# Unscaled first transposes, aligned buffers, later gate sums, 128-row rotary scores and second modulation vectors from the first stage on, in a hybrid attention block

## The chip, the cores and the metric

The kernel runs on one core of a Trainium2 chip. The metric is the device time of one execution in microseconds (us). Engines are named as in the profile: PE (TensorE: matmuls; PEld are its weight loads), DVE (VectorE), ACT (ScalarE), POOL (GpSimd), SP (SyncE, which issues most DMAs). L12 is line 12 of the kernel that a row belongs to; the changed kernel has line numbers of its own.

## The reference

One block over 256 latent tokens `x` and 256 context tokens `ctx`, width 2048, in float32. In short:

```python
sh1, sc1, gt1, sh2, sc2, gt2 = split(silu(c) @ w_mod + b_mod, 6)       # and the same of c_ctx
h  = rmsnorm(x, g_attn) * (1 + sc1) + sh1                                # hc of ctx likewise
cq, ckv, kr, qn, kn, vn, f = split_columns(h @ w_in)                     # and of hc
o_mla = 8 heads: scores of (128 plain + 64 rotary) columns over 512 keys, softmax, values
o_na  = 4 heads of neighbourhood attention with a bias, plus the context keys
o_fn  = Fourier mixing of f in 4 groups
x  = x + gt1 * (concat(o_mla, o_na, o_fn) @ w_out)
h2 = rmsnorm(x, g_ffn) * (1 + sc2) + sh2
u  = depthwise_conv3(h2 @ w_up) + conv_b                                 # 2 x 5632 columns
x  = x + gt2 * ((silu(gate(u)) * val(u)) @ w_down)
return rmsnorm(x, g_final)
```

`w_mod` alone is 2048 x 12288: its first third feeds the first modulation (sh1, sc1), the rest, 67 MB, the gates and the second modulation.

## The kernel before

Every float32 operand of a large product is kept as two fp32r limbs, H (the rounded value, made by ACT, L123) and L (the rest, made by DVE, L124); `split` makes them. A product is then three matmuls, H·H, H·L and L·H (`mm3`, L108 to L111). Weights arrive over SP's queue as `raw` tiles of 1 MB, in the list `order`, some tiles ahead, and are split by quarters into `hl` tiles.

The stages, in the order in which PE goes through them:

- First stage (to about 146 us). `x` and `ctx` come in four tiles of 128 tokens; each is squared and summed on ACT (L299), its rstd is made (L105, L106), the tile is scaled (L301) and transposed by PE (L364, with the identity from `sm`, a constant tile that comes by DMA) into `xT`. Then for each of 16 blocks `g` of 128 channels: `mod1_mm(g)` multiplies silu(c) by 2 MB of `wm1` (L318, into the bank `ms`), ACT copies the sums (`part`, L321), `mod1_h(g)` transposes them (L326), DVE adds them up (`mt`, L330) and the modulated block is written as limbs into `hx` and `hc`; and `g1(g)` accumulates seven output tiles over the channels with `wA`. `mod1_mm(g)` and `mod1_h(g)` are written among the tiles of `g1(g - 1)`; the tile framework orders each engine's instructions by priorities and dependences.
- V, B, NA (to 282 us), F, FN and MLA (to 440): the other projections, neighbourhood attention, Fourier mixing, MLA. In MLA the query of a pair of heads is `q[:, limb, i, :]`: i = 0, 1 are the two heads' plain columns, i = 2 their 64 rotary columns one above the other. A rotary score is an `mm3` with 64 rows of q and of the key `krH`, `krL`.
- O (to 522): the output projection `wo`, in four blocks of 512 columns; `x2_cols` (L742, L743) adds the gated result to x, `h_cols` transposes it (L754) into `h2`, scaled by `A2`. `h2` has two columns more than tokens, which hold the limbs of `B2`.
- UP and DN in four chunks (to the end): the MLP's first matmuls read `h2` with those columns (258 wide). After eight of them `hn`, the finished input, is there, and `up_mm2` runs two matmuls per weight tile: L834 multiplies the weight's H by both limbs of `hn` at once (512 wide), L835 its L by H (256 wide). DN (`at`, then `x2_cols` again) uses `mm3` with 512 columns.

Beside this runs the second modulation, `m2`: 128 tiles `wm2` of 0.5 MB, issued by POOL (L221) into 4 buffers, each multiplied by one element of silu(c) per partition and accumulated on DVE (L234, L236) into `acc`, 16 tiles to a block of 1024 columns, the blocks in the order gate 1, sc2/sh2, gate 2. `paced(n)` counts PE's columns, and with `RATES` of the stage calls `fill()`: one DMA more, one accumulation more, and `m2_sum()` if a block is complete. For a gate block, `m2_end` splits `acc` into limbs `acl` and `m2_sum` sums it over the partitions with a matrix of ones (L270, L271); for the others, eight matmuls of two columns (L260) go to `b2v`, from which `A2` and `B2` are made. `fill_to(n)` finishes n tiles: 64 ahead of `A2`, 96 ahead of `B2` and the added columns of `h2`, 112 and 128 in DN. From the 97th tile on, a small copy on POOL (`hold`, L216) that reads a weight's fresh limb stands ahead of the DMA.

Large tiles share sixteen buffers of 8256 bytes (`b8`), sized by `h2`'s 258 columns.

Of the kernel before, what the change touches and what calls it, by code (L numbers as in the profile page):

```python
# [33 lines left out]
RATES = dict(V=0.647, B=0.336, NA=0.237, F=0.135, FN=0.464, MLA=0.292, O=0.226, UP=0.132, DN=0.428)  # L34
# [18 lines left out]
def block_kernel(ctx: ExitStack, tc: tile.TileContext, a, out):  # L53
# [13 lines left out]
    def b8(shape, dt=F32, s="b8"):  # L67
        return sp.tile(shape, dt, tag="b8", bufs=16, name=nm(s))
# [39 lines left out]
    def mm3(ps, lH, lL, rH, rL, first, last, skip=False):  # L108
        pe.matmul(ps, lH, rH, start=first, stop=False, skip_group_check=skip)  # L109
        pe.matmul(ps, lH, rL, start=False, stop=False, skip_group_check=skip)  # L110
        pe.matmul(ps, lL, rH, start=False, stop=last, skip_group_check=skip)  # L111
        paced(3 * rH.shape[-1])

# [67 lines left out]
    def take(key, i):  # L181

        n = quarters.index((key, i))
        while st[1] <= min(n + look[0], len(quarters) - 1):
# [7 lines left out]
            ins = split(t[:, 0, :hs], t[:, 1, :hs], raws[k][:, o : o + hs])  # L192
# [60 lines left out]
    def m2_sum():
        if m2["due"] is None:
            return
# [12 lines left out]
        for h in range(2):  # L268
            ps = bank()
            pe.matmul(ps, ones_r, v[h][:, 0, :], start=True, stop=False)  # L270
            pe.matmul(ps, ones_r, v[h][:, 1, :], start=False, stop=True)  # L271
# [24 lines left out]
    act.dma_start(rope, a["rope"])
    for t in range(4):
        junk = b8([P, D], s="junk")
        act.activation(junk, xt[t], AF.Square, accum_out=ssx[:, t : t + 1])  # L299
        rstd(rx[:, t : t + 1], ssx[:, t : t + 1], D)  # L300
        dve.tensor_scalar(xt[t], xt[t], rx[:, t : t + 1], None, ALU.mult)  # L301
    act.activation(c1, smv("c1"), AF.Silu)
# [8 lines left out]
    def mod1_mm(g):  # L311

        for q in range(2):
            w = raw_tile(("m", g, q), 6)
            w = w.rearrange("p (k n) -> p k n", k=8)
            for k in range(8):
                r = 32 * (k % 4)
                pe.matmul(ms[r : r + 32, 0:256], cs[:, 8 * q + k, :], w[:, k, :], start=(q == 0 and k < 4),  # L318
                          stop=(q == 1 and k >= 4), tile_position=(0, r))
# [4 lines left out]
    def mod1_h(kt, sb):  # L324
        for s in range(2):
            pe.transpose(ms[:, 256 + s * P : 256 + (s + 1) * P], sb[:, s * P : (s + 1) * P], ident)  # L326
        t = tiny(4, "mt")
        tv = t.rearrange("p (s j) -> p s j", s=2)
        quarters_ = ms[:, 256:512].rearrange("p (s r c) -> p s c r", s=2, r=4)[:, :, 0:2, :]
        dve.tensor_reduce(tv, quarters_, AX.X, ALU.add)  # L330
        dve.tensor_tensor(tv, tv, bm1[:, kt], ALU.add)
        dve.scalar_tensor_tensor(tv[:, 1], tv[:, 1], 1.0, ga[:, kt], ALU.add, ALU.mult)
        m = kt // 4
        if hx[m] is None:
# [15 lines left out]
    def g1(kt, tiles):  # L350
        for i in tiles:
# [5 lines left out]
            mm3(accs[i][:, SEQ:], lH, lL, *hsl(hc, kt), first=False, last=(kt == KT - 1), skip=True)  # L357

    for t in range(4):
        for m in range(4):  # L360
            ps = bank()
            for k in range(4):
                kt = 4 * m + k
                pe.transpose(ps[:, k * P : (k + 1) * P], xt[t][:, kt * P : (kt + 1) * P], ident)  # L364
            (act.copy if m % 2 else dve.tensor_copy)(xT[m][:, :, t * P : (t + 1) * P],
                                                     ps.rearrange("p (k q) -> p k q", k=4))
# [59 lines left out]
    def rope_T(ps, H, L):  # L426
# [5 lines left out]
        split(H, L, r)  # L432
# [3 lines left out]
    rope_T(ps[:, :SEQ], krH[:, :SEQ], krL[:, :SEQ])  # L436
# [610 lines left out]
```

## Time and profile before

| | us |
|---|---|
| median of three runs | 1277.49 (1276.57 to 1278.4) |
| profiled execution | 1279.01 |
| span in the profile | 1277.2 |
| PE busy | 1243.7 (97%) |
| PE weight loads (beside matmuls) | 1069.2 (84%) |
| DVE busy | 978.6 (77%) |
| ACT busy | 699.0 (55%) |
| POOL busy | 111.5 (9%) |
| DMA | 304.81 MB, mean 239 GB/s |

PE is busy nearly all the time. A matmul's end is modelled in the profile, and matmuls overlap at their ends, so the distance from one start to the next tells what a matmul costs, and its mean duration (ns) moves with that distance. In rows of waits the releaser is the instruction that came last.

### The profile page before, as it was taken

What the parts mean: (1) busy time and instruction counts of PE and PEld (TensorE: products, weight loads), DVE (VectorE), ACT (ScalarE), POOL (GpSimd) and SP (SyncE); (2) the same over time, 40 slices, a digit from 0 to 9 for tenths busy, and PEclk for the clock granted to TensorE, in tenths of its full rate; (3) what the DMA queues carried; (4) which work ended last, traced back from release to release, by engine and by line L of the source; (5) the groups of instructions that cost most, each with busy time, mean ns of one, the idle gap of its engine ahead of it and who ended that gap; (6) DMA issues with size and microseconds to landing.
All of it is one profiled execution on the core that took longest, in us unless ns stands there. A gap on an engine that the chain in (4) does not pass through costs nothing.

```text
span 1277.2 us, 19956 instructions
## 1 busy us (share of the span) xinstructions
PE 1243.7 (97%) x7536; PEld 1069.2 (84%) x7536; DVE 978.6 (77%) x1757; ACT 699.0 (55%) x1343; POOL 111.5 (9%) x177
## 2 busy tenths in 40 slices
PE   5999999999999999999999999999999999999996
PEld 4888879898787888999988878888888888888885
DVE  5444588999989788899989975777766677777785
ACT  5333323765555555576666544666654566556663
POOL 0000121111111002200121500000000000000000
PEclk9999999999999999999999999999999999999999
DMA  9998689677756977754767857544455645564531
GB/s 387 419 397 327 223 305 323 231 243 249 258 194 232 368 294 270 261 227 165 286 226 253 320 204 264 212 162 169 165 198 180 249 165 183 184 227 165 172 125 66
DMA packets 53648, 304.81 MB, mean 239 GB/s; under 512 B 6064, under 2 KB 7216, under 8 KB 26800
## 3 DMA queue, kind: packets, MB, share of 16 engines
q1 hardware_dynamic: 34256, 234.37, 49.7%
q0 software_dynamic: 18432, 67.12, 15.5%
q10 hardware_dynamic: 864, 2.05, 0.4%
q8 instruction: 59, 0.97, 0.3%
q14 instruction: 37, 0.30, 0.1%
HBM read 301.42 MB, written 2.10 MB: 238 GB/s over the span
## 4 chain that ended last, share of the span: by engine, by line
PE 90%; DMA 3%; DVE 3%; issue 1%; ACT 1%; POOL 0%; DVEq 0%; ACTq 0%; POOLq 0%
PE ps L834 21%; PE ps L109 16%; PE ps L110 15%; PE ps L111 15%; PE ps L835 11%; DMA wm<-in_wm_dram 3%; PE g L109 2%; PE ms L318 2%; PE g L110 2%; PE g L111 2%; DVE acc L236 1%; DVE hl L124 1%; PE ps L493 1%; PE ps L364 1%; DMA sm<-in_small_dram 1%
## 5 line engine op out<-in xcount | busy, mean ns | idle before, releaser
L123 ACT CAST hl<-raw 128x512 fp32r<-128x512 f32 (+2 forms) x732 | 444.0, 611 | 359.8 <-PE ps L111 191.1
L124 DVE TENSOR_TENSOR hl<-raw,hl 128x512 fp32r<-128x512 f32 (+2 forms) x732 | 485.8, 677 | 172.6 <-ACT hl L123 166.4
L834 PE MATMUL ps<-hn,hl 128*128 128x512 f32 x1152 | 404.3, 395 | 0.0
L835 PE MATMUL ps<-hn,hl 128*128 128x256 f32 x1152 | 323.4, 281 | 0.0
L834 PEld LDWEIGHTS ps<-hn,hl 128*128 128x128 f32 x1152 | 216.4, 188 | 51.2
L835 PEld LDWEIGHTS ps<-hn,hl 128*128 128x128 f32 x1152 | 217.1, 188 | 0.2
L236 DVE SCALAR_TENSOR_TENSOR acc<-wm,c,acc 128x1024 f32<-128x1024 f32 x120 | 153.6, 1280 | 8.7 <-DMA wm<-in_wm_dram 8.4
L110 PE MATMUL ps<-hl,act 128*128 128x512 f32 x344 | 135.7, 394 | 0.5 <-DVE hl L124 0.5
L109 PE MATMUL ps<-hl,act 128*128 128x512 f32 x344 | 135.2, 393 | 0.0
L111 PE MATMUL ps<-hl,act 128*128 128x512 f32 x344 | 135.2, 393 | 0.0
L221 POOL DMA_DIRECT2D wm<-in_wm_dram x128 | 68.3, 534 | 310.7 <-DVE acc L236 233.8
L110 PEld LDWEIGHTS ps<-hl,act 128*128 128x128 f32 x344 | 64.7, 188 | 15.9 <-DVE hl L124 1.5
L109 PEld LDWEIGHTS ps<-hl,act 128*128 128x128 f32 x344 | 64.6, 188 | 14.9
L111 PEld LDWEIGHTS ps<-hl,act 128*128 128x128 f32 x344 | 64.7, 188 | 14.6
L109 PE MATMUL ps<-h,hl 128*128 128x258 f32 x256 | 72.5, 283 | 0.0
L111 PE MATMUL ps<-h,hl 128*128 128x258 f32 x256 | 72.1, 282 | 0.0
L110 PE MATMUL ps<-h,hl 128*128 128x258 f32 x256 | 72.1, 282 | 0.0
L216 POOL COPY hold<-hl 128x1 f32<-128x1 f32 x36 | 36.0, 999 | 286.7 <-DVE hl L124 286.7
L109 PE MATMUL ps<-hl,mix 128*128 128x512 f32 x128 | 50.5, 394 | 0.0
L110 PE MATMUL ps<-hl,mix 128*128 128x512 f32 x128 | 50.1, 391 | 0.0
L111 PE MATMUL ps<-hl,mix 128*128 128x512 f32 x128 | 49.9, 390 | 0.0
L855 ACT ACTIVATE cv<-ps,sm 128x256 f32<-128x256 f32 x88 | 49.4, 564 | 0.5
(282 smaller groups left out, 2143.2 us busy)
## 6 DMA issues: line engine op xcount, KB each, us to landing
raw<-in_wup_dram SPq DMA_DIRECT2D x88, 1024.0 KB, 5.1
wm<-in_wm_dram POOLq DMA_DIRECT2D x128, 512.0 KB, 5.1
raw<-in_wdn_dram SPq DMA_DIRECT2D x44, 1024.0 KB, 4.9
raw<-in_wm_dram SPq DMA_DIRECT2D x32, 1024.0 KB, 14.4
raw<-in_wo_dram SPq DMA_DIRECT2D x16, 1024.0 KB, 9.9
raw<-in_wB_dram SPq DMA_DIRECT2D x10, 1024.0 KB, 7.4
raw<-in_wA_dram SPq DMA_DIRECT2D x8, 896.0 KB, 14.5
x<-in_x_dram SPq DMA_DIRECT2D x4, 1024.0 KB, 8.8
```

What stands on the lines that cost most here:

```text
L109: pe.matmul(ps, lH, rH, start=first, stop=False, skip_group_check=skip)
L110: pe.matmul(ps, lH, rL, start=False, stop=False, skip_group_check=skip)
L111: pe.matmul(ps, lL, rH, start=False, stop=last, skip_group_check=skip)
L123: act.copy(H, src)
L124: return dve.tensor_tensor(L, src, H.bitcast(F32), ALU.subtract).ins
L216: hold = pool.tensor_copy(tiny(1, "hold"), recent[0][:, 1, 0:1].bitcast(F32)).ins
L221: pool.dma_start(w, a["wm2"][blk * 16 + kt])
L236: dve.scalar_tensor_tensor(m2["a"], w, c1[:, kt : kt + 1], m2["a"], ALU.mult, ALU.add)
L318: pe.matmul(ms[r : r + 32, 0:256], cs[:, 8 * q + k, :], w[:, k, :], start=(q == 0 and k < 4), stop=(q == 1 and k >= 4), tile_position=(0, r))
L834: pe.matmul(ps, w[:, 0, k * P : (k + 1) * P], h[:, :, k, :], start=kt == 0, stop=False, skip_group_check=True)
L835: pe.matmul(ps[:, :SEQ], w[:, 1, k * P : (k + 1) * P], h[:, 0, k, :], start=False, stop=kt == KT - 1, skip_group_check=True)
L855: act.activation(t, ps[:, :SEQ], AF.Identity, bias=c[:, 3:4], scale=c[:, 1:2])
```

## The change

- x and ctx come in eight half tiles. Their transposes take them unscaled, with an identity `idt` made on the chip by POOL. The square sums make one joint rms: a matmul with ones spreads it over the partitions (`rxb`), and each block of `xT` is multiplied by it on DVE in `mod1_h`. `sm`, `rope` and `c1` come later. All copies out of PE's transposes are DVE's.
- `issue_after` pins orders: the first modulation's matmuls behind the transposes, the joint matmul behind `mod1_mm(0)`, each later `mod1_mm` behind the last `g1`. `G1_CUT` is 2. The tiles of `wA` come as two halves.
- `RATES` has an entry A: some 12 `wm2` tiles are loaded and accumulated in the first stage; V, B and NA have lower rates; F to DN are as before.
- A gate block's limbs are two tiles of 1024 columns, and its sum waits for six more calls of `m2_sum` (`SUM_LAG`) or for `fill_to`.
- The buffers are 12 of `b8` (8192 bytes) and 4 of `h8` (8448 bytes, for `h2`, x, q, k and others). `hn` is stored by channel block, then limb, so that L834's 512 columns are one run.
- A rotary query is stored with H in one half of the partitions and L in the other, for each head; a score takes two matmuls of 128 rows (with `krH`, `krL`, which hold the key twice) instead of three of 64.

```diff
-RATES = dict(V=0.647, B=0.336, NA=0.237, F=0.135, FN=0.464, MLA=0.292, O=0.226, UP=0.132, DN=0.428)
+RATES = dict(A=0.17, V=0.45, B=0.2, NA=0.16, F=0.135, FN=0.464, MLA=0.292, O=0.226, UP=0.132, DN=0.428)
...
     def b8(shape, dt=F32, s="b8"):
-        return sp.tile(shape, dt, tag="b8", bufs=16, name=nm(s))
+        return sp.tile(shape, dt, tag="b8", bufs=12, name=nm(s))
+    def h8(shape, dt=F32, s="h8"):
+        return sp.tile(shape, dt, tag="h8", bufs=4, name=nm(s))
...
     def m2_end(blk, acc):
         if KIND[blk // 2] != "g":
-            m2["due"] = (blk, acc)
+            m2["due"], m2["age"] = (blk, acc), SUM_LAG
             return
...
+        H, L = [sp.tile([P, 1024], F32R, tag="acc", bufs=3, name=nm("acl")) for _ in range(2)]
+        split(H, L, acc)
+        m2["due"], m2["age"] = (blk, (H, L)), 0
+
+    def m2_sum(now=False):
+        m2["age"] += 1
+        if m2["due"] is None or not (now or m2["age"] > SUM_LAG):
             return
...
     def fill_to(n):
-        while m2["acc"] < n or m2["due"]:
+        while m2["acc"] < n:
             fill()
+        m2_sum(True)
...
+    def x_in():
+        for t in range(4):
+            for h in range(2):
+                junk = sp.tile([P, 1024], F32, tag="acc", bufs=3, name=nm("junk"))
+                last = act.activation(junk, xt[t][:, h * 1024 : (h + 1) * 1024], AF.Square,
+                                      accum_out=ssx[:, 2 * t + h : 2 * t + h + 1]).ins
+                for m in (2 * h, 2 * h + 1):
+                    ps = bank()
+                    for k in range(4):
+                        kt = 4 * m + k
+                        pe.transpose(ps[:, k * P : (k + 1) * P], xt[t][:, kt * P : (kt + 1) * P], idt)
+                    copied = dve.tensor_copy(xT[m][:, :, t * P : (t + 1) * P], ps.rearrange("p (k q) -> p k q", k=4)).ins
+        x_made.extend([last, copied])
+        with tc.issue_after(last):
             act.dma_start(sm, a["small"])
...
+        ps = bank()
+        with tc.issue_after(m_mm[0]):
+            x_made.append(pe.matmul(ps, ones, dgs, start=True, stop=True).ins)
+        x_made[0] = act.copy(rxb, ps).ins
...
+            if g:
+                held.enter_context(tc.issue_after(g1_last[-1]))
...
+            dve.tensor_tensor(xk, xk, rxb, ALU.mult)
...
+    def qr_limbs(q):
+        def limbs(src):
+            for i, hs in enumerate(halves):
+                act.copy(q[hs, i, 2, :], src[hs])
+            for i, hs in enumerate(halves):
+                dve.tensor_tensor(q[halves[1 - i], i, 2, :], src[hs], q[hs, i, 2, :].bitcast(F32), ALU.subtract)
+        return limbs
...
-            mm3(ps, q[hs, 0, 2, qs], q[hs, 1, 2, qs], krH[hs, :], krL[hs, :], False, True)
+            pe.matmul(ps, q[:, i, 2, qs], krH, start=False, stop=False)
+            pe.matmul(ps, q[:, i, 2, qs], krL, start=False, stop=True)
...
-    h2 = [b8([P, 2, 4, SEQ + 2], F32R, s="h2") for _ in range(4)]
+    h2 = [h8([P, 2, 4, SEQ + 8], F32R, s="h2") for _ in range(4)]
...
-        hn.append(b8([P, 2, 4, SEQ], F32R, s="hn"))
+        hn.append(b8([P, 4, 2, SEQ], F32R, s="hn"))
...
-                pe.matmul(ps, w[:, 0, k * P : (k + 1) * P], h[:, :, k, :], start=kt == 0, stop=False, skip_group_check=True)
+                pe.matmul(ps, w[:, 0, k * P : (k + 1) * P], h[:, k].rearrange("p s n -> p (s n)"), start=kt == 0, stop=False, skip_group_check=True)
```

In the order of the instructions this shows at three places. The first is PE at the end of the transposes of x. Before (`raw_41` to `raw_46` are tiles of `wm1`, two to a block; `part` the copied sums):

```order
L364 MATMUL ps_33_209<-sm_64,x_8_90 128x128 x4
L318 MATMUL ms_17_118<-raw_41_222,cs_72 32x256 x8
L318 MATMUL ms_17_118<-raw_42_224,cs_72 32x256 x8
L326 MATMUL ms_17_118<-sm_64,part_49_254 128x128 x2
L318 MATMUL ms_17_118<-raw_44_228,cs_72 32x256 x8
L318 MATMUL ms_17_118<-raw_45_230,cs_72 32x256 x8
L326 MATMUL ms_17_118<-sm_64,part_58_294 128x128 x2
L318 MATMUL ms_17_118<-raw_46_232,cs_72 32x256 x8
```

PE there, after (L347 is the joint rms, `g1_0` the first accumulator of `g1`):

```order
L327 MATMUL ps_39_215<-idt_72,x_8_93 128x128 x4
L367 MATMUL ms_15_108<-raw_9_96,cs_74 32x256 x8
L367 MATMUL ms_15_108<-raw_10_98,cs_74 32x256 x8
L347 MATMUL ps_46_252<-dgx_45_250,ones_r_68 128x512
L379 MATMUL ms_15_108<-idt_72,part_43_244 128x128 x2
L116 MATMUL g1_0_47_255<-hx_55_269,hl_59_279 128x256
```

Two and a half blocks of the modulation stood ahead of the first `g1` matmul; now one does, with the joint matmul.

The second is PE in V, around the first gate sum (`acl` the accumulator's limbs, `hl` a quarter of a V weight). Before:

```order
L109 MATMUL ps_197_1619<-hl_230_1798,hx_159_1270 128x512
L110 MATMUL ps_197_1619<-hl_230_1798,hx_159_1270 128x512
L111 MATMUL ps_197_1619<-hl_230_1798,hx_159_1270 128x512
L270 MATMUL ps_246_1898<-acl_240_1877,ones_r_68 128x512
L271 MATMUL ps_246_1898<-acl_240_1877,ones_r_68 128x512
L270 MATMUL ps_247_1902<-acl_241_1880,ones_r_68 128x512
L271 MATMUL ps_247_1902<-acl_241_1880,ones_r_68 128x512
L109 MATMUL ps_198_1620<-hl_230_1798,hc_160_1271 128x512
```

PE in V after:

```order
L116 MATMUL ps_217_1690<-hl_245_1858,hx_176_1314 128x512
...
L118 MATMUL ps_218_1691<-hl_245_1858,hx_176_1314 128x512
...
L118 MATMUL ps_219_1692<-hl_245_1858,hc_177_1315 128x512
L286 MATMUL ps_257_1949<-acl_239_1830,ones_r_68 128x512
L287 MATMUL ps_257_1949<-acl_240_1831,ones_r_68 128x512
L286 MATMUL ps_258_1953<-acl_239_1830,ones_r_68 128x512
L287 MATMUL ps_258_1953<-acl_240_1831,ones_r_68 128x512
```

The sum now stands behind nine matmuls with `hl_245`; on DVE the limbs `acl` are made two instructions ahead of that `hl_245`.

The third is the seam between `wo` and the MLP. PE before (`acc_729` is the block of sh2, `hl_849` the last `wo` weight, `x2_743` the second half of the tokens, `hl_851` a weight of the MLP):

```order
L111 MATMUL ps_823_5234<-hl_837_5304,mix_541_3737 128x512
L260 MATMUL ps_845_5353<-ones_r_68,acc_729_4666 128x2 x8
L109 MATMUL ps_824_5235<-hl_837_5304,mix_541_3737 128x512
...
L111 MATMUL ps_824_5235<-hl_849_5372,mix_684_4454 128x512
L754 MATMUL ps_862_5438<-sm_64,x2_743_4759 128x128
L754 MATMUL ps_863_5447<-sm_64,x2_743_4759 128x128
L109 MATMUL ps_867_5481<-h2_745_4766,hl_851_5383 128x258
```

PE after:

```order
L118 MATMUL ps_821_5234<-hl_839_5349,mix_682_4459 128x512
L826 MATMUL ps_852_5416<-sm_64,x2_738_4746 128x128
...
L826 MATMUL ps_853_5425<-sm_64,x2_739_4747 128x128
L276 MATMUL ps_862_5454<-ones_r_68,acc_773_4929 128x2 x8
L116 MATMUL ps_866_5489<-h2_740_4753,hl_842_5363 128x258
```

The sum of the block of sh2 stood inside the `wo` matmuls; now it stands between the last of them and the first MLP matmul. On POOL, before, a `hold` copy and a DMA take turns:

```order
L221 DMA wm2_805_5104<-in_wm2_dram 128x1024
L216 COPY hold_810_5139<-hl_809_5129 128x1
L221 DMA wm2_811_5141<-in_wm2_dram 128x1024
L216 COPY hold_827_5245<-hl_826_5238 128x1
L221 DMA wm2_828_5247<-in_wm2_dram 128x1024
```

POOL after (`wm2_849` is the 96th tile, the last that the sum of `acc_773` needs; `hl_848` is a quarter of an MLP weight):

```order
L239 DMA wm2_840_5359<-in_wm2_dram 128x1024
L234 COPY hold_854_5435<-hl_848_5387 128x1
L234 COPY hold_856_5440<-hl_848_5387 128x1
L234 COPY hold_858_5445<-hl_848_5387 128x1
L234 COPY hold_860_5450<-hl_848_5387 128x1
L239 DMA wm2_849_5400<-in_wm2_dram 128x1024
L239 DMA wm2_855_5437<-in_wm2_dram 128x1024
```

Four copies that read one MLP weight now stand in a row ahead of the last DMA of the 96.

More of the change, by code (lines that the diff above doesn't have):

```diff
@@ L110, in mm3 @@
         pe.matmul(ps, lH, rL, start=False, stop=False, skip_group_check=skip)
-        pe.matmul(ps, lL, rH, start=False, stop=last, skip_group_check=skip)
+        ins = pe.matmul(ps, lL, rH, start=False, stop=last, skip_group_check=skip).ins
         paced(3 * rH.shape[-1])
+        return ins
     def paced(n):
@@ L191, in take @@
             t = quarter(k)
-            ins = split(t[:, 0, :hs], t[:, 1, :hs], raws[k][:, o : o + hs])
+            with ExitStack() as held:
+                if k == ("A", 0):
+                    for made in x_made if q < 2 else (hx_made[-1], hmade[-1]):
+                        held.enter_context(tc.issue_after(made))
+                ins = split(t[:, 0, :hs], t[:, 1, :hs], raws[k][:, o : o + hs])
             hls[k, q] = recent[0] = t
@@ L293, in block_kernel @@
         xt.append(x_)
-        if t == 0:
-            act.dma_start(sm, a["small"])
[L296 to L302, printed above, removed]
+    emit_dma(order.index(("m", 1, 1)))
+    hmade, hx_made, g1_last, m_mm, x_made = [], [], [], [], []
@@ L311, in mod1_mm @@
     def mod1_mm(g):
[L313 to L319, printed above, removed]
+        with ExitStack() as held:
+            if g:
+                held.enter_context(tc.issue_after(g1_last[-1]))
+            for q in range(2):
+                w = raw_tile(("m", g, q), 6)
+                w = w.rearrange("p (k n) -> p k n", k=8)
+                for k in range(8):
+                    r = 32 * (k % 4)
+                    ins = pe.matmul(ms[r : r + 32, 0:256], cs[:, 8 * q + k, :], w[:, k, :], start=(q == 0 and k < 4),
+                                    stop=(q == 1 and k >= 4), tile_position=(0, r)).ins
+                m_mm.append(ins)
         sb = b1(s="part")
@@ L324, in mod1_h @@
     def mod1_h(kt, sb):
[L325 to L330, printed above, removed]
+        with ExitStack() as held:
+            for made in g1_last[-1:] if kt else x_made[1:]:
+                held.enter_context(tc.issue_after(made))
+            for s in range(2):
+                pe.transpose(ms[:, 256 + s * P : 256 + (s + 1) * P], sb[:, s * P : (s + 1) * P], idt)
+            t = tiny(4, "mt")
+            tv = t.rearrange("p (s j) -> p s j", s=2)
+            quarters_ = ms[:, 256:512].rearrange("p (s r c) -> p s c r", s=2, r=4)[:, :, 0:2, :]
+            dve.tensor_reduce(tv, quarters_, AX.X, ALU.add)
         dve.tensor_tensor(tv, tv, bm1[:, kt], ALU.add)
@@ L356, in g1 @@
             mm3(accs[i][:, :SEQ], lH, lL, *hsl(hx, kt), first=(kt == 0), last=(kt == KT - 1), skip=True)
[L357 to L366, printed above, removed]
+            g1_last.append(mm3(accs[i][:, SEQ:], lH, lL, *hsl(hc, kt), first=False, last=(kt == KT - 1), skip=True))
+    x_in()
+    sb0 = mod1_mm(0)
+    x_rms()
     accs = [bank(f"g1_{i}") for i in range(N_A)]
     for g in range(KT):
+        if g == 0:
+            mod1_h(0, sb0)
+            continue
+        if g == 1:
+            g1(0, range(0, 4))
+            with tc.issue_after(hx_made[-1]):
+                act.dma_start(rope, a["rope"])
+                act.activation(c1, smv("c1"), AF.Silu)
+            pace[0] = RATES["A"]
         sb = mod1_mm(g)
-        if g:
-            g1(g - 1, range(0, G1_CUT))
+        n = 5 if g == 1 else G1_CUT
+        g1(g - 1, range(4 if g == 1 else 0, n))
         mod1_h(g, sb)
-        if g:
-            g1(g - 1, range(G1_CUT, N_A))
+        g1(g - 1, range(n, N_A))
     g1(KT - 1, range(N_A))
@@ L431, in rope_T @@
         dve.tensor_tensor(r, r, sw, ALU.add)
-        split(H, L, r)
+        limbs(r)
+    def qr_limbs(q):
[5 more added lines that the diff above has]
+        return limbs
     ps = bank()
     proj_T(("B", 1), ps, True)
-    rope_T(ps[:, :SEQ], krH[:, :SEQ], krL[:, :SEQ])
+    rope_T(ps[:, :SEQ], lambda r: split(krH[:, :SEQ], krL[:, :SEQ], r))
     split(krH[:, SEQ:], krL[:, SEQ:], ps[:, SEQ:])
```

80 lines of the change are left out of this document (49 added, 31 removed).

## The prediction

> **What bounds the kernel now.** I read the page first, then TensorE's waits, then stages in windows, then single places in the timeline.
>
> ```profile
> PE 1243.7 (97%) x7536; PEld 1069.2 (84%) x7536; DVE 978.6 (77%) x1757; ACT 699.0 (55%) x1343; POOL 111.5 (9%) x177
> ...
> PE 90%; DMA 3%; DVE 3%; issue 1%; ACT 1%; POOL 0%; DVEq 0%; ACTq 0%; POOLq 0%
> ...
> L834 PE MATMUL ps<-hn,hl 128*128 128x512 f32 x1152 | 404.3, 395 | 0.0
> ...
> L110 PE MATMUL ps<-hl,act 128*128 128x512 f32 x344 | 135.7, 394 | 0.5 <-DVE hl L124 0.5
> ...
> L216 POOL COPY hold<-hl 128x1 f32<-128x1 f32 x36 | 36.0, 999 | 286.7 <-DVE hl L124 286.7
> ```
>
> TensorE (PE) works 1243.7 of the span's 1277.2 us and is 90% of the chain that ended last. So only three things can move the end: the 33.5 us in which PE is idle, the number of matmuls, and the time of one. The profiled execution took 1279.01 us, 1.5 above the median of the three runs, 1277.49. I sum against the profiled one and take 1.5 off at the end. The runs lie within 1.83 us, so 0.2% (2.6 us) is about what can be told from no change.
>
> TensorE's waits (line, what it waited for, us in total, times, longest):
>
> ```profile
> PE ps L364 <- DVE v L105: 13.6, 1, 13.6
> PE ps L270 <- ACT acl L123: 3.8, 2, 2.9
> PE ms L326 <- ACT part L321: 2.5, 5, 0.5
> PE ms L318 <- DVE mt L330: 1.9, 5, 0.5
> ```
>
> 13.6 us pass before the first transpose; nearly all the other waits are in the two places that the change rewrites, the modulation's matmuls of the first stage and the gate sums.
>
> **1. The first stage.** Windows (us; busy PE, PEld, DVE, ACT, POOL; granted clock, DMA share, GB/s) and PE's timeline:
>
> ```profile
> 0.00:10.00 10.00, 0.00 (x0) 0.00 (x0) 0.67 (x3) 2.17 (x4) 0.20 (x4) 1.00 0.81 313
> 14.00:24.00 10.00, 10.00 (x71) 9.75 (x73) 8.77 (x13) 7.17 (x12) 1.38 (x3) 1.00 1.01 419
> 54.00:84.00 30.00, 29.17 (x305) 24.38 (x304) 12.45 (x36) 9.68 (x20) 0.00 (x0) 1.00 1.00 409
> ```
>
> ```profile
> 23.74 1.93 PE L318 MATMUL ms<-raw,cs 128*32 128x256 f32 x32
> 26.17 0.44 PE L326 MATMUL ms<-sm,part 128*128 128x128 f32 x2 [0.49 <-ACT part L321]
> 26.94 1.93 PE L318 MATMUL ms<-raw,cs 128*32 128x256 f32 x32 [0.34 <-DVE mt L330]
> 30.33 1.07 PE L318 MATMUL ms<-raw,cs 128*32 128x256 f32 x16 [0.52 <-DVE mt L330]
> 31.33 0.74 PE L109 MATMUL g<-hx,hl 128*128 128x256 f32 x4
> ```
>
> Before, the transposes wait for the squares, the rstd and the scaling of x, and for `sm`, which carries the identity. After, they wait for a half tile of x alone. What then holds the first modulation matmul is its weight: x (4.2 MB) and the first pair of `wm1` tiles (2.1 MB) are 6.3 MB, and the windows give 3.1 MB by 10 us and 0.42 MB per us behind it, so 17.6 us; I say 18.5, since `sa` comes in beside them. With 1.93 us for the matmuls, and 4 us for part, transposes, the joint rms matmul, the scaling of the first block and its two limbs (four to five short steps like the 26.17 to 26.94 one), `g1(0)` starts near 24.5 instead of 31.33. Of those 6.8 us, `mm(1)` and half of `mm(2)`, 1.93 + 1.07 us, and transposes of 0.44 now lie behind it: 3.4 are won. Of the 4.4 us of waits at L326 and L318, 1.84 lie ahead of 31.33 (they are in those 6.8), and the other 2.6 go, because every `mod1_mm` now stands behind all of `g1` and its transposes two `g1` tiles later, so the ACT copy and the DVE sum run under other matmuls. -6.0. What is late next is the DMA: a step of `g` takes about 7.3 us (30 us windows hold four, less the wait) and now loads 2.1 MB of `wm1`, 0.46 of `wA` and 0.8 tiles (0.4 MB) of `wm2`, 2.96 MB, or 0.41 MB per us, where these windows delivered 0.409 to 0.419. There is no slack left; I give 1 us back. DVE gets sixteen products of 128x512 and twelve accumulations of 1.28 us, some 25 us over a stage in which it was busy 12.45 of 30: hidden. **-5** (0 to -8).
>
> **2. The gate sum in V.** PE's timeline, and the clock:
>
> ```profile
> 183.35 0.60 PE L270 MATMUL ps<-acl,ones_r 128*128 128x512 f32 x1 [2.88 <-ACT acl L123]
> 184.08 0.80 PE L271 MATMUL ps<-acl,ones_r 128*128 128x512 f32 x1
> ...
> 187.14 0.39 PE L110 MATMUL ps<-hl,hc 128*128 128x512 f32 x1
> ```
>
> ```profile
> 180.00:190.00 10.00, 6.99 (x24) 5.01 (x23) 9.42 (x12) 2.28 (x4) 2.28 (x5) 0.83 0.82 272
> ```
>
> PE idles 2.88 us until the accumulator's limbs are there, and then runs at a lower clock (0.83 in this window): from the wait's begin at 180.47 to 187.14 stand eight matmuls, which at 0.23 us each are 1.84 us of 6.67. The late sum has its limbs long before PE comes to it, and the barrier is not a wait any more. **-4.8** (-3 to -5). The limbs' split of 1024 columns is the same DVE and ACT work. The other one of L270's two waits, 0.9 us, is that of DN, where the sum likewise moves back, with its broken rhythm behind it: **-1.4** (0 to -1.5).
>
> **3. The rotary scores.** One query tile of one pair of heads, PE's timeline:
>
> ```profile
> 425.50 0.40 PE L111 MATMUL ps<-kh,qh 128*128 128x512 f32 x1
> 425.83 0.50 PE L109 MATMUL ps<-krH,qh 64*128 64x512 f32 x1
> 426.17 0.40 PE L110 MATMUL ps<-krL,qh 64*128 64x512 f32 x1
> 426.40 0.39 PE L111 MATMUL ps<-krH,qh 64*128 64x512 f32 x1
> 426.72 0.51 PE L109 MATMUL ps<-kh,qh 128*128 128x512 f32 x1
> 427.06 0.40 PE L110 MATMUL ps<-kh,qh 128*128 128x512 f32 x1
> ```
>
> Between 128-row matmuls starts are 0.23 us apart. Where rows go from 128 to 64 the step is 0.33 and the first 64-row one takes 0.34; back to 128 again 0.32 and 0.34. So a tile pays 0.10 + 0.11 + 0.09 + 0.11 for the two changes of shape, and 0.23 for the third matmul, all of which go: 0.64 x 16 = 10.2, of which I take **-9.5** (if only the matmuls go, 16 x 0.23 = -3.7). `qr_limbs` issues two 64-row copies and two subtractions for one of each, under the next head's work.
>
> **4. Buffers and the order of `hn`.** A buffer of 8256 bytes is 32 x 256 + 64, so sixteen of them start at four places modulo 256 bytes. In DN the left operand `at` lies in one such buffer and the weights in others:
>
> ```profile
> 780.73 0.40 PE L110 MATMUL ps<-hl,act 128*128 128x512 f32 x1
> ...
> 781.20 0.39 PE L109 MATMUL ps<-hl,act 128*128 128x512 f32 x1
> ...
> 783.01 0.39 PE L111 MATMUL ps<-hl,act 128*128 128x512 f32 x1
> ```
>
> The groups of 781.2 to 783.2 us, and of 950.8 to 953.2 us (L109 alone):
>
> ```profile
> L109 PE MATMUL ps<-hl,act 128*128 128x512 f32 x3 | 1.2, 389 | 0.0
> ...
> L109 PE MATMUL ps<-hl,act 128*128 128x512 f32 x4 | 1.6, 395 | 0.0
> ```
>
> From 781.20 to 783.01 are eight steps from start to start, 226 ns each; there both operands' buffers begin at byte 32 modulo 256 (addresses of the built program). The two steps before 781.20, with 32 against 160, are 235 ns. The groups say the same: 389 ns, and 395 at 950 us, again 32 against 160. After the change all these buffers begin at 32. DN's 1032 matmuls have a mean of 394, so 5 ns each to go, -5.2; some 1000 other 512-wide ones I put at -1.3 together. L834, 1152 of them, reads `hn` as two runs of 256 at 395 ns in the mean; as one run of 512 it should come to 389: -6.9. The 256-wide ones at equal starts I put at 2 ns more, +4. **-9.5** (-17 to +4).
>
> The Trainium skill, "TensorE: Matmul & The Clock Gate", Part 2 (on LDWEIGHTS), says that PE has two independent SBUF read ports and that loading the next tile's weights takes no read bandwidth from the running matmul. By that rule the place of the two buffers cannot matter and term 4 would be 0. The step at 781.20 speaks against it, but only for the pair of buffers seen there.
>
> **5. From the output projection to the MLP.** The last of `wo`, and what follows (PE, then POOL, then VectorE, DVE):
>
> ```profile
> 521.57 0.39 PE L111 MATMUL ps<-hl,mix 128*128 128x512 f32 x1
> ...
> 521.94 0.37 PE L109 MATMUL ps<-h,hl 128*128 128x258 f32 x1
> ```
>
> ```profile
> 522.09 1.18 POOL L216 COPY hold<-hl 128x1 f32<-128x1 f32 x1 [6.08 <-DVE hl L124]
> 523.52 0.53 POOL L221 DMA_DIRECT2D wm<-in_wm_dram  x1 [0.25 <-DVE acc L236]
> ```
>
> ```profile
> 512.84 1.48 PE L260 MATMUL ps<-ones_r,acc 128*128 128x2 f32 x12
> ...
> 521.94 1.28 DVE L236 SCALAR_TENSOR_TENSOR acc<-wm,c,acc 128x1024 f32<-128x1024 f32 x1
> ...
> DMA to landing us min/median/max: 3.9/5.6/7.0
> ```
>
> Now MLP matmuls follow without a gap, because the 96th `wm2` tile was summed (L260, 512.84) while `wo` still ran. The change takes 12 tiles into stage 1 but cuts V, B and NA by more, and O's rate is as it was; in the new order the last tiles of the 96, their sum, `B2` and the two added columns of `h2` stand behind the last `wo` matmul, and the first MLP matmul reads those columns. The 96th tile's DMA stands on POOL behind four hold copies, which wait for the split of a weight at about 522. From there: four copies at their mean of 1.0, 4.0; issue 0.53; landing 5.6; accumulation 1.28; eight matmuls of the sum, 1.0; copy, `B2`, limbs, some 1.9: 14.3 us, so the MLP starts near 536.3 instead of 521.94. What moved into that gap is 2.0 us of transposes and sums that PE did elsewhere, and the clock after so long an idle time costs 1.7 us if it goes as at 183 us. **+14** (+8 where the copies fit into DVE's pauses and the tile lands in 3.9; +19 with a landing of 7.0 and copies of 2 us).
>
> **Sum.** -5 -4.8 -1.4 -9.5 -9.5 +14 = -16.2: 1279.0 - 16.2 = 1262.8, less 1.5 for the median: **1261 us**.
>
> **Rivals.**
> A. The seam is cheap: the tile's DMA is out before the copies, and the wait is under 4 us. For it: POOL is busy 9%, and a copy alone is short. Against it: the order on POOL is fixed. 1261 - 12 = 1249.
> B. Buffer places and runs do nothing: PE's reads of the two operands don't meet, and the differences of term 4 come from elsewhere in those stages, so that it is 0: 1261 + 9.5 = 1270. For it: L834 is the one shape of which the trace has no contiguous row.
> C. Stage 1 is bound by the DMA: at 0.409 instead of 0.419 MB per us some 51 MB take 3 us longer than counted, and each `wm2` tile that POOL puts among the SP queue's ones delays the `wm1` tile PE needs: term 1 becomes +3, 1269.
> D. Slower than before: equal starts make PE's two reads meet instead of keeping them apart, so that the step of 9 ns at 781.20 goes the other way for the shapes seen nowhere at equal starts in long stretches, L834 above all. At half of it for the 1152 of L834 and the 2040 other 512-wide ones that is +14, with +4 from the 256-wide ones: 1261 + 9.5 + 18 = 1288. It decides from 0.9 ns a matmul, where 3192 x 0.9 + 4 use up the other terms' -6.7, and from 1.7 ns with the margin of 0.2%. Against it stands the stretch after 781.20.
> E. The change does not do what it says in the rotary part (the switch to and from 64 rows is paid elsewhere): 1261 + 6 = 1267.
>
> **Chances.** Forecast (1255 to 1266) 0.42; A 0.20; B 0.16; C 0.07; E 0.06; D 0.07; 0.02 for no change. All but D and the 0.02 are faster by over 2.6 us: faster 0.90, same 0.03, slower 0.07. The range holds the forecast, A, B, C and E with the seam's upper end: 1246 to 1273.
>
> **What the profile after would show.** Term 1: the first transposes near 6 to 8 us, `g1` from about 24.5, no waits of the `ms` matmuls in the stage, DMA share 1.0 until some 125 us. Term 2: no gate sum among PE's waits, granted clock 1.00 around 180 us. Term 3: 32 rotary matmuls of 128 rows near 390 ns each instead of 48 of 64. Term 4: L906 near 389 ns instead of 395, 512-wide ones all near 389. Term 5: an idle time of PE of 10 to 14 us behind the last `wo` matmul, ended by the limbs of `h2`, with a lower clock behind it. The prediction would be wrong if that gap is missing or twice as long, or if L906 has not moved.

## The result: 0.6% slower, and the profile after

The changed kernel takes 1286.41 us (median of six runs, 1283.34 to 1289.12), the one before 1278.62 in runs beside it: a ratio of 1.0063, 95% interval 1.0044 to 1.0081. It is slower, where I had put 0.90 on faster. The profiled execution took 1286.14 us, 7.1 more than that of before. Experiment 9's figure below is the median of three runs; its fourth took 4289 us and is left out, without a cause on record.

The page of the changed kernel (busy time; chain; the MLP's two matmuls):

```profile
PE 1242.3 (97%) x7522; PEld 1081.2 (84%) x7522; DVE 991.3 (77%) x1776; ACT 699.2 (54%) x1344; POOL 108.2 (8%) x175
...
PE 90%; DMA 5%; DVE 2%; ACT 1%; POOL 1%; issue 1%; DVEq 0%; POOLq 0%; SPq 0%; ACTq 0%
...
L906 PE MATMUL ps<-hn,hl 128*128 128x512 f32 x1152 | 405.5, 397 | 0.0
L907 PE MATMUL ps<-hn,hl 128*128 128x256 f32 x1152 | 323.3, 281 | 0.0
```

PE is as busy as before (1242.3 against 1243.7 us) although 16 matmuls are gone, and it idles 42 us instead of 33.5. Its waits, and three windows:

```profile
PE ps L327 <- DMA x<-in_x_dram: 5.2, 1, 5.2
PE ps L276 <- DVE s L854: 4.8, 1, 4.8
PE ms L379 <- ACT part L371: 4.6, 1, 4.6
PE ps L826 <- DVE x L815: 3.5, 1, 3.5
PE ps L117 <- DVE hl L132: 2.9, 1, 2.9
PE g L116 <- ACT hx L401: 2.4, 1, 2.4
```

```profile
20.00:40.00 20.00, 12.93 (x90) 9.15 (x91) 7.44 (x19) 6.05 (x13) 1.28 (x2) 0.77 1.02 416
500.00:520.00 20.00, 14.30 (x64) 11.47 (x62) 17.74 (x25) 9.17 (x18) 4.58 (x10) 0.88 1.00 405
520.00:540.00 20.00, 16.07 (x101) 15.87 (x102) 8.62 (x26) 4.58 (x14) 2.08 (x3) 0.69 0.28 104
```

The old waits (the gate sum in V, the pairs of 0.5 us at the modulation, and all but 5.2 of the 13.6 us for the first transpose) have gone as foreseen. New ones stand in two places: 7 us of idle time between 20 and 40 us, and nearly 10 us between 510 and 530, each with a lower granted clock (0.77, 0.69). Where the stages begin, by PE's timeline, after and then before:

```profile
150.21 0.40 PE L116 MATMUL ps<-hl,hx 128*128 128x512 f32 x1
...
322.13 0.40 PE L739 MATMUL ps<-krH,qh 128*128 128x512 f32 x1
...
512.15 0.39 PE L118 MATMUL ps<-hl,mix 128*128 128x512 f32 x1
...
527.47 0.80 PE L116 MATMUL ps<-h,hl 128*128 128x258 f32 x2 [1.34 <-ACT h L131]
...
622.71 0.40 PE L906 MATMUL ps<-hn,hl 128*128 128x512 f32 x1
```

```profile
145.31 0.39 PE L109 MATMUL ps<-hl,hx 128*128 128x512 f32 x1
...
322.75 0.49 PE L109 MATMUL ps<-krH,qh 64*128 64x512 f32 x1
...
615.20 0.40 PE L834 MATMUL ps<-hn,hl 128*128 128x512 f32 x1
```

With 521.57 and 521.94 for the seam before, the lengths differ like this:

| stretch | predicted | measured |
|---|---|---|
| first stage (to V's first matmul) | -5 | +4.9 |
| V to the first rotary score | -4.8 | -5.5 |
| rotary scores to the last `wo` matmul | -9.5 | -8.8 |
| last `wo` matmul to the MLP's first | +14 with the clock | +15.0 |
| the MLP's 258-wide matmuls | in the +14 | +2.0 |
| the rest (pairs of L906 and L907, DN) | most of term 4's -9.5, and -1.4 | -0.3 |

Two terms of the sum failed, the first stage and the buffers. The experiments go through the places in turn. Their ratios stand against the kernel before in runs beside them, 1280.4 to 1280.6 us. The changed kernel stands in one set of runs only, beside 1278.62, so a difference from its 1286.41 can be off by some 2 us; the traces say where it lies.

### The profile page after: what moved, and what is told of

It reads as the page before. It is cut to its first block, busy times and chain, and to the rows that moved or that the text cites. A ratio compares the mean times of both kernels' runs of the same rounds, so it can differ in the third digit from the quotient of the medians.

```text
span 1284.4 us, 19953 instructions
## 1 busy us (share of the span) xinstructions
PE 1242.3 (97%) x7522; PEld 1081.2 (84%) x7522; DVE 991.3 (77%) x1776; ACT 699.2 (54%) x1344; POOL 108.2 (8%) x175
## 4 chain that ended last, share of the span: by engine, by line
PE 90%; DMA 5%; DVE 2%; ACT 1%; POOL 1%; issue 1%; DVEq 0%; POOLq 0%; SPq 0%; ACTq 0%
PE ps L906 20%; PE ps L116 16%; PE ps L117 16%; PE ps L118 16%; PE ps L907 10%; PE g L116 2%; PE ms L367 2%; PE g L117 2%; PE g L118 2%; DMA wm<-in_wm_dram 2%; DMA raw<-in_wA_dram 1%; PE ps L565 1%; POOL hold L234 1%; DMA x<-in_ctx_dram 1%; PE ps L276 1%
## 5 line engine op out<-in xcount | busy, mean ns | idle before, releaser
L906 PE MATMUL ps<-hn,hl 128*128 128x512 f32 x1152 | 405.5, 397 | 0.0
L907 PE MATMUL ps<-hn,hl 128*128 128x256 f32 x1152 | 323.3, 281 | 0.0
L906 PEld LDWEIGHTS ps<-hn,hl 128*128 128x128 f32 x1152 | 216.2, 188 | 52.4
L907 PEld LDWEIGHTS ps<-hn,hl 128*128 128x128 f32 x1152 | 217.6, 189 | 0.1
L116 PE MATMUL ps<-h,hl 128*128 128x258 f32 x256 | 73.3, 287 | 1.3 <-ACT h L131 1.3
L118 PE MATMUL ps<-h,hl 128*128 128x258 f32 x256 | 73.7, 288 | 0.0
L117 PE MATMUL ps<-h,hl 128*128 128x258 f32 x256 | 73.2, 286 | 0.0
L116 PEld LDWEIGHTS ps<-h,hl 128*128 128x128 f32 x256 | 49.8, 195 | 1.4 <-ACT h L131 1.4
L116 PE MATMUL ps<-hl,mix 128*128 128x512 f32 x128 | 50.3, 393 | 0.0
L118 PE MATMUL ps<-hl,mix 128*128 128x512 f32 x128 | 49.9, 390 | 0.0
```

The lines of the kernel that those rows point to most:

```text
L118: ins = pe.matmul(ps, lL, rH, start=False, stop=last, skip_group_check=skip).ins
L906: pe.matmul(ps, w[:, 0, k * P : (k + 1) * P], h[:, k].rearrange("p s n -> p (s n)"), start=kt == 0, stop=False, skip_group_check=True)
L907: pe.matmul(ps[:, :SEQ], w[:, 1, k * P : (k + 1) * P], h[:, k, 0, :], start=False, stop=kt == KT - 1, skip_group_check=True)
```

## Experiments

**1. The rotary scores alone.** The kernel before, with `qr_limbs` and these lines in `mla_scores`:

```diff
-            mm3(ps, q[hs, 0, 2, qs], q[hs, 1, 2, qs], krH[hs, :], krL[hs, :], False, True)
+            pe.matmul(ps, q[:, i, 2, qs], krH, start=False, stop=False)
+            pe.matmul(ps, q[:, i, 2, qs], krL, start=False, stop=True)
```

> The kernel before with the 128-row rotary scores alone. Theory: from the first rotary score to the last output-projection matmul it gains what the changed kernel gained there, 8.8 us (-7.5 to -10). But the two new matmuls are written without mm3, so their 16 x 1536 columns no longer count in paced(): 10.5 us x 0.292 = 3 tiles of wm2 are not called for in MLA. By the theory that this is one cause of the gap at the MLP, the sum of the 96th tile now stands behind the last wo matmul and the MLP's first matmul starts 5 to 8 us after that last one instead of 0.4: total -1 to -4 us against before. Rival (the gap comes from the lower rates of V, B and NA alone): no gap, total -8 to -9.5.

1284.1 us, ratio 1.0037 (1.0024 to 1.005): the scores, which the traces show as 11 us shorter from the first of them to the last `wo` matmul, make the kernel slower, where -1 to -4 us was expected. PE at the seam of this run, whose last `wo` matmul starts at 510.19:

```profile
513.71 2.99 PE L260 MATMUL ps<-ones_r,acc 128*128 128x2 f32 x16 [2.90 <-DVE acc L236]
...
518.82 0.58 PE L109 MATMUL ps<-h,hl 128*128 128x258 f32 x1 [0.74 <-ACT h L123]
```

The gap is 8.6 us, a little over the expected 5 to 8. It is the wm2 sum that came late, because a matmul that is written without `mm3` no longer advances `paced()`: ahead of the last `wo` matmul DVE had started 94 accumulations, against 97 before. Another 6 us lie behind it, 1.7 in the 258-wide matmuls and the rest in the pairs and DN.

**2. The same scores, counted.** One line more, `paced(3 * 512)`, behind the two matmuls of a score.

> The kernel before with the rotary scores of 128 rows alone, and with their columns counted in paced() as those of the three matmuls were (3 x 512 a score). Theory (the gap at the MLP in the run with the scores alone came from the uncounted columns): the sum of the 96th wm2 tile is back inside wo, no gap, and the scores' 9 to 11 us are left: total -8.5 to -11 against before. Rival (the faster MLA stage itself leaves the wm2 tiles too little time): a gap of 3 us or more, total -4 to -7.

1273.21 us, ratio 0.9933 (0.991 to 0.9957), 7.4 us faster than before. The trace has no gap at the seam (0.37 us as before) and 9.3 us less between the first score and the last `wo` matmul; V's first matmul comes 1.8 us later, with a wait of 1.5 us for a `wm1` tile in the first stage, and the first rotary score another 1.4, so the gain falls short of the expected 8.5 to 11. The two kernels differ in that one line: an uncounted helper call is the difference between 0.4% slower and 0.7% faster.

**3. The changed kernel, counted.** The same line in the changed kernel.

> The changed kernel with the rotary scores' columns counted in paced(). Theory: the uncounted columns (3 tiles) and the lower rates of V, B and NA (the rest) both make the 96 tiles late; with 3 tiles more the gap at the MLP shrinks from 15 to 6 to 9 us, as with the rates of before: total -6 to -9 against the changed kernel, 1278 to 1280. Rival (the uncounted columns alone): no gap, 1270.

1278.83 us: 7.6 less than the changed kernel, and a gap of 8.8 us is left. Both causes are needed to explain the 15 us. Ahead of the last `wo` matmul DVE had started 97 accumulations before and 91 in the changed kernel; it is 94 here and 94 with the rates of before (experiment 5): three tiles by the uncounted columns, three by the lower rates.

**4. A higher rate in O.** `O=0.226` becomes `O=0.33`.

> The changed kernel with the rate of O at 0.33 instead of 0.226, nothing else; the sum of the 96th wm2 tile then stands inside the wo matmuls. Theory: the 15 us between the last wo matmul and the MLP's first, and some 2 us of low clock behind it, are the price of the 96 tiles being late: 1286.4 - 15 to -17 = 1270 (1267 to 1273). Rival (the transfer and the four hold copies only move, or DVE, at 67 of 82 us in O, gets late with the weights' limbs): 1276 or more.

1270.06 us, ratio 0.9928 (0.9912 to 0.9945). PE at the seam:

```profile
514.44 0.39 PE L118 MATMUL ps<-hl,mix 128*128 128x512 f32 x1
514.67 0.38 PE L826 MATMUL ps<-sm,x 128*128 128x128 f32 x2
514.81 0.60 PE L116 MATMUL ps<-h,hl 128*128 128x258 f32 x3
```

No gap is left; the late tiles cost some 16 us in all.

**5. The rates of before.** `A=0.0, V=0.647, B=0.336, NA=0.237` in the changed kernel.

> The changed kernel with RATES as before (A = 0, V 0.647, B 0.336, NA 0.237): no wm2 tile in the first stage. Theory (ACT's queue): the first stage loses the same 4 to 7 us at 29 to 39 us, with 0 to 2 us less since 1 MB of wm2 is out of the way. Rival (the wm2 tiles delay wA): block 3's mm starts near 43 us instead of 50.15. At the MLP: by the uncounted rotary columns 2 or 3 of the 96 tiles are still missing, so a gap of 5 to 8 us instead of 15. Total 1274 to 1280 by the theory, 1269 to 1272 by the rival.

1278.48 us. The block-3 matmul of the modulation starts at 48.39 us instead of 50.15, so the `wm2` tiles of the first stage are not what stalls it. The gap at the seam is 7.4 us. V to the first rotary score is 7.3 us longer than in the changed kernel, without any wait for a gate sum. V itself is as short (44.6 us from its first matmul to the first 256-wide one behind it, against 44.7); the difference lies behind it, with 6.0 us of waits instead of 3.8, and its cause was not followed further.

**6. ACT's order in the first stage.** The limbs of `wA` are held behind the copy that PE waits for:

```diff
+                if k[0] == "A" and k[1]:
+                    held.enter_context(tc.issue_after(parts[2 * k[1]]))
                 ins = split(t[:, 0, :hs], t[:, 1, :hs], raws[k][:, o : o + hs])
...
-        act.copy(sb, ms[:, 0:256])
+        parts.append(act.copy(sb, ms[:, 0:256]).ins)
```

> The changed kernel with the limbs of wA tile n (n from 1 on) held behind the ACT copy part of block 2n; nothing else. Theory: PE's wait of 4.6 us at 34 us, with the low clock behind it, comes from ACT's queue, where part of block 1 stands behind three casts of a wA tile whose two halves land at 35.4 and 37.8 us: mm of block 3 starts near 44 instead of 50.15 us, total -5 to -7 us (1280). Rival (the stage is bound by the DMA, and the tile's landing sets the time anyway): block 3 no earlier than 48.5, total -0 to -2.

1281.9 us, 4.5 less than the changed kernel, a little short of the expected 5 to 7. ACT's timeline of the changed kernel shows the cause, with the PE row that waits:

```profile
35.44 1.03 ACT L131 CAST hl<-raw 128x512 fp32r<-128x512 f32 x2 [5.67 <-DMA raw<-in_wA_dram]
37.75 0.62 ACT L131 CAST hl<-raw 128x512 fp32r<-128x512 f32 x1 [1.28 <-DMA raw<-in_wA_dram]
38.27 0.36 ACT L371 COPY part<-ms 128x256 f32<-128x256 f32 x1
...
38.69 0.69 PE L379 MATMUL ms<-idt,part 128*128 128x128 f32 x2 [4.61 <-ACT part L371]
```

The sums were ready in `ms` at about 33 us; their copy stood behind three casts of a `wA` tile that nobody needed yet and that landed at 35.4 and 37.8. With the order pinned, ACT and PE, and then the block-3 matmul with the edit, in the changed kernel and before:

```profile
32.89 0.37 ACT L374 COPY part<-ms 128x256 f32<-128x256 f32 x1 [2.67 <-PE ms L370]
...
33.45 0.38 PE L382 MATMUL ms<-idt,part 128*128 128x128 f32 x2
```

```profile
42.26 0.42 PE L370 MATMUL ms<-raw,cs 128*32 128x256 f32 x4
...
50.15 0.42 PE L367 MATMUL ms<-raw,cs 128*32 128x256 f32 x4
...
42.81 0.42 PE L318 MATMUL ms<-raw,cs 128*32 128x256 f32 x4
```

V's first matmul comes at 143.85 instead of 150.21 us, 1.5 earlier than before. That is what the first stage's part of the change is worth without the stall, not the 5 us of my term 1. `g1(0)` starts at 24.80 us, 6.5 earlier than before and close to the 24.5 of the sum. But PE has waited 5.5 us in three pieces between 16 and 25 us, only one of them (1.5) for a weight's DMA, and then runs at a lower clock (the window, and two rows of `g1(0)`):

```profile
20.00:30.00 10.00, 7.44 (x44) 6.09 (x45) 3.68 (x11) 3.91 (x8) 0.00 (x0) 0.71 1.02 416
...
27.10 0.41 PE L117 MATMUL g<-hc,hl 128*128 128x256 f32 x1
27.32 0.41 PE L118 MATMUL g<-hc,hl 128*128 128x256 f32 x1
```

The `g1` matmuls start 0.21 us apart there instead of 0.12, which costs some 2.7 us by block 3. Later one step between blocks takes 8.8 us instead of 7.3, behind a `wA` tile that lands at 56.8 us; the DMA share is 1.0 in the stage.

**7. Both edits together.** The changed kernel with the edits of experiments 4 and 6.

> The changed kernel with both edits, O's rate at 0.33 and the limbs of wA behind part. Theory: the two gaps are separate places, so their gains add: -16 for the gap at the MLP and -5 for the first stage, 1286.4 - 21 = 1265 (1262 to 1268). Rival (the earlier finish of stage 1 is given back in a later wait for weights or wm2 tiles): 1270, as with O's rate alone.

1264.81 us, ratio 0.9875 (0.9852 to 0.9899). The gains add, as expected. This kernel is the base of the following ones.

**8. No lag of the gate sums.** `SUM_LAG = 0`.

> As the kernel with both edits, with SUM_LAG at 0, so that each gate sum stands where PE comes to it with the next call of fill. Theory (the later sum is what removed the wait in V): PE waits for the accumulator's limbs in V again, 2 to 3 us and the lower clock behind it: +3 to +5.5 between V's first matmul and the first rotary score, total +3 to +6. Rival (the lower rate of V did it, the limbs being ready earlier): 0 to +1.

1270.68 us, 5.9 more than with both edits, inside the expected total but not where the theory put it. V is as short as with the lag (44.7 us, against 50.5 before). The wait is in DN, at 728.5 us, and DN's first stretch is 4.9 us longer:

```profile
PE ps L288 <- ACT acl L131: 3.7, 1, 3.7
```

So the lag is worth 5 us in DN. In V the lower rate alone removes the wait, and so does the lag alone, with the rates of before (experiment 5).

**9. The order of `hn` undone.** `hn` as `[P, 2, 4, SEQ]`, L906's operand as two runs of 256, buffers aligned.

> As the kernel with both edits, but hn stored as before, so that L906's 512 columns are two runs of 256, in aligned buffers. Theory (one run of 512 is worth something of its own): the pair's step in the first chunk is 350 to 356 ns instead of 346.7, +1 to +2.4 us there, and in the other chunks 350 to 356 too. Rival (the order of hn does nothing): 346.7 in the first chunk and 353.3 in the others, total the same as with both edits.

1266.55 us. The pairs of L906 and L907 are timed best from a chunk's first pair to DN's first matmul. In the second chunk these are 384 pairs; before, after, and here:

```profile
797.73 0.39 PE L834 MATMUL ps<-hn,hl 128*128 128x512 f32 x1
...
932.44 0.39 PE L109 MATMUL ps<-hl,act 128*128 128x512 f32 x1
```

```profile
805.57 0.39 PE L906 MATMUL ps<-hn,hl 128*128 128x512 f32 x1
...
941.24 0.40 PE L116 MATMUL ps<-hl,act 128*128 128x512 f32 x1
```

```profile
786.35 0.39 PE L909 MATMUL ps<-hn,hl 128*128 128x512 f32 x1
...
922.02 0.40 PE L116 MATMUL ps<-hl,act 128*128 128x512 f32 x1
```

That is 350.8 ns a pair before, 353.3 after, and 353.3 with the old order; in the first chunk, where a gate sum stands ahead of DN and the steps from pair to pair are counted instead, 346.7 both with the new order and with the old. One run of 512 or two of 256 makes no difference at all. (The trace is 2.1 us longer than the base's. 1.6 of that lies between the first rotary score and the last `wo` matmul, a stretch that differs by 3 us, 191.9 to 195.1, among the kernels with both edits, without an edit there.)

**10. Buffers not aligned.** `b8` with 16 buffers of 8256 bytes, no `h8`.

> As the kernel with both edits, but with the buffers as before: sixteen of 8256 bytes, at four places modulo 256. Theory: 512-wide matmuls go back from 226.7 to 230 to 233 ns (DN and the projections, +5 to +8 us together), the 256- and 258-wide ones from 120 to 117 to 119 (-3 to -4), the pairs of the last three chunks from 353.3 to 351 (-2), those of the first from 346.7 to 351 (+1): total +1 to +4. Rival (aligned buffers are worth what I predicted, 5 us or more): +5 to +10. Rival (they are worth nothing or less): -3 to 0.

1269.33 us, 4.5 more than the base, a little above the theory's 1 to 4; in the traces 3.7 of it lie in DN. DN's matmuls in the second chunk, before, after and here:

```profile
L109 PE MATMUL ps<-hl,act 128*128 128x512 f32 x79 | 31.2, 395 | 0.0
```

```profile
L116 PE MATMUL ps<-hl,act 128*128 128x512 f32 x82 | 31.9, 389 | 0.0
```

```profile
L116 PE MATMUL ps<-hl,act 128*128 128x512 f32 x73 | 28.6, 392 | 0.0
```

So alignment does what I read at 781 us for the 512-wide matmuls that follow each other, and 256-wide ones lose by it (283 ns against 278 to 280 in the windows from 200 us on). For the pairs it gives either 346.7 or 353.3 ns, against 351.7 here.

**11. Another entry into the pairs.** On the base, with a matmul or three whose result nobody reads ahead of a chunk:

```diff
+        for w in {1: [256], 2: [258], 3: [258] * 3}.get(ci, []):
+            pe.matmul(bank()[:, :w], ones_r, hn[0][:, 0].rearrange("p s n -> p (s n)")[:, :w], start=True, stop=True)
```

> As the kernel with both edits, and one or more matmuls whose result nobody reads ahead of the MLP's first matmul in the chunks after the first: one of 256 columns in the second, one of 258 in the third, three of 258 in the fourth. In the changed kernel a pair of the 512- and the 256-wide matmul (L906, L907) takes 346.7 ns from start to start in the first chunk and 353.3 in the three others, in one repeating pattern each. Theory: with all buffers aligned the stream locks into one of two phases, set by where it enters; another entry puts at least one of the three chunks at 346.7: -2.6 us in the second chunk or -1.7 in the third or fourth, against 0.1 to 0.4 for the added matmuls. Rival (the first chunk is faster because of what else runs beside it, the wm2 transfers and sums): 353.3 in all three, total +0.6.

1264.42 us. The second and fourth chunk stay at 353.3 ns a pair; the third, 256 pairs, with one matmul of 258 columns ahead, does not:

```profile
985.29 0.40 PE L909 MATMUL ps<-hn,hl 128*128 128x512 f32 x1
...
1074.04 0.40 PE L116 MATMUL ps<-hl,act 128*128 128x512 f32 x1
```

88.75 us are 346.7 ns a pair, where the changed kernel and the base have 90.44 (353.3). The base differs here in nothing but the added matmul, so the entry sets the step, and it holds for the whole chunk. The total does not show it: 0.4 us are within the spread of the runs.

**12. That entry in all chunks.** `{1: [258], 2: [258], 3: [258]}`.

> As the kernel with both edits, with one matmul of 258 columns whose result nobody reads ahead of the MLP's first matmul in the second, third and fourth chunk. Theory (the phase is set by the entry, which one of 258 columns put right in the third chunk): 346.7 ns a pair in all chunks, -2.6 -1.7 -1.7 + 0.3: 1264.8 - 5.7 = 1259 (1257 to 1261.5). Rival (the phase at the entry differs from chunk to chunk, so that the same addition helps in one alone): 1263.

1259.27 us, ratio 0.9835 (0.981 to 0.9861) against the kernel before. The second chunk:

```profile
782.78 0.28 PE L965 MATMUL ps<-hn,ones_r 128*128 128x258 f32 x1
782.89 0.40 PE L909 MATMUL ps<-hn,hl 128*128 128x512 f32 x1
...
916.02 0.40 PE L116 MATMUL ps<-hl,act 128*128 128x512 f32 x1
```

346.7 ns a pair in all four chunks, 5.9 us less in the traces of the three that have the added matmul. This version beats both kernels: 21.4 us under the one before.

## Why the prediction was wrong

- **Term 1, the first stage (-5, measured +4.9): the step that failed.** The order of the instructions on ACT was not followed. I wrote that with the transposes two `g1` tiles later the copy `part` runs under other matmuls; it stood behind three casts that wait for a DMA (experiment 6, 6.4 us to V's first matmul). Rival C, the DMA by way of the `wm2` tiles, fell (experiment 5): mm of block 3 moved by 1.8 us without them. The gain itself was also too high: 1.5 us with the stall removed. `g1(0)` came as early as I had it, but the sum had no lower clock behind the short waits ahead of it; that takes 2.7 of the 3.4 us won there (experiment 6). The steps between blocks did shorten in the changed kernel, from 133.07 - 42.81 to 137.95 - 50.15 us over twelve blocks, by the 2.5 us that I had (2.6); with the stall removed by 0.9 only.
- **Term 2, the gate sums (-4.8 and -1.4).** V lost its wait, and -5.5 us is left at the first rotary score. The mechanism was right, but in V the lower rate does the same without the lag (experiment 8). In DN the lag is worth 5 us, yet in the changed kernel a wait of 2.9 us for a weight's limbs took its place. It goes with the late tiles: 2.3 us with half of them (experiment 3) and none without (experiment 4), where DN's first stretch is 2 us shorter than before.
- **Term 3, the rotary scores (-9.5, measured -8.8).** Right, and alone -9.3 (experiment 2) or -11.0 (experiment 1). What the term lacked is that `mm3` also paces the `wm2` tiles. I gave the lateness to the rates alone; experiments 1 and 3 show that the rotary edit is about half of it.
- **Term 4, the buffers (-9.5; undoing them cost 4.5 in experiment 10): the other step that failed.** The -5.2 for DN came, a little smaller: its last three stretches are 2.8 us shorter, 4.4 ns for each of their 648 matmuls where I had 5; the first one's gain is hidden by the wait of term 2. The -6.9 for L906 did not come: its mean is 397 ns, not 389. I took the difference of 6 ns between 395 and 389 for the price of two runs; experiment 9 shows that the runs cost nothing, and that pairs in aligned buffers have a step set by their entry, 353.3 in three chunks and 346.7 in one. Rival D's direction was right for those three chunks, at 2.5 ns a pair and not 4.5 a matmul, some 2 us in all; that its 1288 lies close to the measured time is luck. Rival B was right about the runs and wrong about the places. The Trainium skill, "TensorE: Matmul & The Clock Gate", Part 2, has two independent read ports and no interference between weight loads and the moving operand. By that the places of the buffers would cost nothing; they cost 4.5 us between experiments 7 and 10. Which access meets which was not settled, nor why the entry sets the step.
- **Term 5, the seam (+14, measured +15.0, and 2.0 behind it).** The place and the cause were right, the parts not: the four copies took 1.46 us instead of 4.0, issue and landing up to the accumulation 7.05 instead of 6.1, the eight matmuls of the sum 3.54 at the low clock instead of 1.0. Rival A, a wait under 4 us, fell. POOL, DVE and PE of the changed kernel:

```profile
512.70 1.46 POOL L234 COPY hold<-hl 128x1 f32<-128x1 f32 x4 [4.92 <-DVE hl L132]
514.11 0.54 POOL L239 DMA_DIRECT2D wm<-in_wm_dram  x1
...
521.16 1.28 DVE L254 SCALAR_TENSOR_TENSOR acc<-wm,c,acc 128x1024 f32<-128x1024 f32 x1 [0.39 <-DMA wm<-in_wm_dram]
...
522.59 3.54 PE L276 MATMUL ps<-ones_r,acc 128*128 128x2 f32 x16 [4.83 <-DVE s L854]
```

  Behind the seam some 20 of the 258-wide matmuls start 0.21 us apart instead of 0.12 before the clock is back, which is about the 2.0 us. With no gap (experiment 4) that is gone, and the stretch is still 1.9 us longer than before: a wait of 1.4 us for limbs of `h2` stands in it instead.
- **The sum.** -16.2 was forecast and +7.1 measured: 9.9 from term 1, 10.6 in the pairs and DN (term 4 for L906, and DN's new wait), 3 at the seam. Nine tenths on faster was too much for a sum in which one term of +14 stood against gains from single rows: 6 ns of a group of 1152 was carried from one shape to another without a row of that shape.

## What to carry to other kernels

A helper that also keeps count (of columns, of turns) is part of the schedule: an edit that goes around it moves work elsewhere, here 8 to 11 us for 16 scores. Where a change moves when something is loaded, follow the order of the instructions on every engine that touches the load: here an early cast that waited for a DMA held up the copy behind it by some 5 us, and PE with it. And a mean duration of a group is not a property of its shape; before it is carried over, look whether the group has more than one step and what sets it.

## What the runs showed of the hardware

A stream of 512- and 256-wide matmuls with all operands at one place modulo 256 bytes falls into a repeating pattern with one of two mean steps, 346.7 or 353.3 ns a pair, and stays in it for 130 us; one matmul of 258 columns at the entry changes it, one of 256 or three of 258 did not. With operands at four places the pairs of the second chunk average 350.0 to 352.5 (experiments 1, 2 and 10 and the kernel before). Matmuls of 512 columns that follow each other (DN's second stretch) start 226.7 ns apart on average with operands at one place, and 230.1 to 233.3 at four. After three waits of 1.4 to 2.6 us between 16 and 25 us the granted clock was 0.71 over the window from 20 to 30 us, and matmuls of 256 columns started 0.21 us apart instead of 0.12 (experiment 6).
